# Rotary embedding on one core: the sum of the two products moves from VectorE to TensorE and ScalarE, and all x transfers become whole 4 MB chunks

## The chip, the core and the metric

The kernel runs on one core of a Trainium2 chip. The metric is the device time of one execution in microseconds. A profile of one execution is at hand; its span runs from the first to the last instruction, and the execution's own time is a little longer than the span.

## The reference

The kernel applies rotary position embedding to x of shape (16, 512, 1024), float32, with 16 heads of 64 numbers each. cos and sin have the shape (512, 32) and are shared by all batches and heads.

```python
x = x.reshape(batch, seq, num_heads, head_dim)
x1, x2 = x[..., :half_dim], x[..., half_dim:]
cos = cos[None, :, None, :]; sin = sin[None, :, None, :]
rotated = concatenate([x1*cos - x2*sin, x1*sin + x2*cos], axis=-1)
```

Input and output are 33.5 MB each.

## The kernel before

**Tiling.** A *unit* is one sequence row per partition: 128 partitions x 1024 numbers (16 heads x 2 halves x 32), 512 KB. There are 64 units. A *group* `g` is four batches; within it each partition holds `R = 16` consecutive sequence rows of one batch. Units are loaded and stored in *chunks* of 1, 2, 4 or 8 units: the first group is cut 1, 1, 2, 4, 8, the last 8, 4, 2, 1, 1, those between 8, 8, so there are 14 chunks. A chunk of n units is one DMA with n x 4 KB contiguous bytes per partition.

**Ring.** `x_sb` holds 40 units. The result overwrites x in place, and the store goes out of the same slots. The loads are issued from SP's queue (L86), which waits, before a load into used slots, for the store that empties them (L85). The stores are issued from ACT's queue (L101).

**Work of a unit.** Three steps, on two engines:

- GpSimd (POOL) multiplies the swapped halves of x by the table of -sin and +sin into `t2_sb`, one instruction for each half (L121, 128x512). `t2_sb` has `NT2 = 4` buffers.
- VectorE (DVE) multiplies x by cos into PSUM, `t1_ps` with `NT1 = 3` slots (L147, 128x1024).
- VectorE adds the two products back into x's place in SBUF (L160, 128x1024). It lags the cosine product by `LEAD = 2` units, in the written order of the loop at the end.

**Tables.** cos and sin are loaded into `stage` from ACT's queue (L90, L91). ScalarE spreads the sine table over the partitions (L97, L98), and VectorE the cosine table into PSUM (L134).

**Order.** The order on each engine is the written one. Engines are kept in step by semaphores alone: `sem_in[c]` (chunk c has landed), `sem_p` (POOL's product), `sem_m` (cosine product), `sem_v` (the sum, which frees buffers and releases stores) and `sem_out[c]` (chunk c is stored).

Of the kernel before, what the change touches and what calls it, by code (L numbers as in the profile page):

```python
# [6 lines left out]
def bass_split_heads_rope_kernel(  # L7
    nc: bass.Bass,
    x: bass.AP,
    cos: bass.AP,  # L10
    sin: bass.AP,
    num_heads: bass.AP,
    out: bass.AP,
):

    batch, seq, dim = x.shape
    H = int(num_heads)
    HD = dim // H  # L20
    HALF = HD // 2
    P = 128
    R = 16
    SB = seq // R
    BL = P // SB
    G = batch // BL
    assert SB * R == seq and BL * SB == P and G * BL == batch and SB == 32

    fp32 = mybir.dt.float32
    mult = mybir.AluOpType.mult  # L30
    add = mybir.AluOpType.add
    COPY = mybir.ActivationFunctionType.Copy


    sizes = [[1, 1, 2, 4, 8]] + [[8, 8]] * (G - 2) + [[8, 4, 2, 1, 1]]
    RING = 40
    chunks = []
    at = 0
    for g, ss in enumerate(sizes):
        r = 0  # L40
        for n in ss:
            slot = at % RING
            assert slot + n <= RING
            chunks.append((g, r, n, slot, at))
            r += n
            at += n
        assert r == R
    NC = len(chunks)
    NU = at
    unit_chunk = []  # L50
    for c, (_, _, n, _, _) in enumerate(chunks):
        unit_chunk += [c] * n

    NT1 = 3
    NT2 = 4

    with ExitStack() as stack:  # L57
        x_sb = stack.enter_context(nc.sbuf_tensor([P, RING, H, 2, HALF], fp32))
        t2_sb = stack.enter_context(nc.sbuf_tensor([P, NT2, H, 2, HALF], fp32))
        stage = stack.enter_context(nc.sbuf_tensor([SB, 2, R * HALF], fp32))  # L60
        s_sb = stack.enter_context(nc.sbuf_tensor([P, R, 2, HALF], fp32))
        c_ps = stack.enter_context(nc.psum_tensor([P, R, HALF], fp32))
        t1_ps = stack.enter_context(nc.psum_tensor([P, NT1, 2 * H, HALF], fp32))
        sem_in = [stack.enter_context(nc.semaphore(f"in{c}")) for c in range(NC)]
        sem_out = [stack.enter_context(nc.semaphore(f"out{c}")) for c in range(NC)]
        sem_cos = stack.enter_context(nc.semaphore("cos"))
        sem_sin = stack.enter_context(nc.semaphore("sin"))
        sem_c = stack.enter_context(nc.semaphore("ctab"))
        sem_s = stack.enter_context(nc.semaphore("stab"))
        sem_p = stack.enter_context(nc.semaphore("pool"))  # L70
        sem_m = stack.enter_context(nc.semaphore("mul"))
        sem_v = stack.enter_context(nc.semaphore("comb"))
        block = stack.enter_context(nc.Block(no_gpsimd_drain=False))

        xv = x.rearrange("(g b) (s r) d -> g (b s) r d", b=BL, r=R)
        ov = out.rearrange("(g b) (s r) h d -> g (b s) r (h d)", b=BL, r=R)
        xs = x_sb[:].rearrange("p n h t d -> p n (h t d)")

        @block.sync
        def _(sp):  # L80
            for c, (g, r, n, slot, at) in enumerate(chunks):
                for e, (_, _, m, eslot, eat) in enumerate(chunks):
                    if eat < at and eat + RING >= at and eslot < slot + n and slot < eslot + m:
                        if eat + RING < at + n and eat + m + RING > at:
                            sp.wait_ge(sem_out[e], 16)  # L85
                sp.dma_start(xs[:, slot:slot + n, :], xv[g, :, r:r + n, :]).then_inc(sem_in[c], 16)  # L86

        @block.scalar
        def _(ae):
            ae.dma_start(stage[:, 0, :], cos.rearrange("(s r) d -> s (r d)", r=R)).then_inc(sem_cos, 16)  # L90
            ae.dma_start(stage[:, 1, :], sin.rearrange("(s r) d -> s (r d)", r=R)).then_inc(sem_sin, 16)  # L91
            ae.wait_ge(sem_sin, 16)
            sv = stage[:, 1, :].rearrange("s (r d) -> s r d", d=HALF)
            for lo, hi in ((0, 4), (4, R)):
                for q in range(BL):
                    ps = slice(q * SB, (q + 1) * SB)
                    ae.activation(s_sb[ps, lo:hi, 0, :], sv[:, lo:hi, :], COPY, scale=-1.0)  # L97
                    ae.activation(s_sb[ps, lo:hi, 1, :], sv[:, lo:hi, :], COPY).then_inc(sem_s, 1)  # L98
            for c, (g, r, n, slot, at) in enumerate(chunks):
                ae.wait_ge(sem_v, at + n)  # L100
                ae.dma_start(ov[g, :, r:r + n, :], xs[:, slot:slot + n, :]).then_inc(sem_out[c], 16)  # L101
            for c in range(NC):
                ae.wait_ge(sem_out[c], 16)

        @block.gpsimd
        def _(pl):
            for u in range(NU):
                c = unit_chunk[u]
                g, r0, n, slot, at = chunks[c]
                r = r0 + u - at  # L110
                k = slot + u - at
                if u == at:
                    pl.wait_ge(sem_in[c], 16)
                if u == 0:
                    pl.wait_ge(sem_s, BL)  # L115
                if r == 4 and g == 0:
                    pl.wait_ge(sem_s, 2 * BL)
                if u >= NT2:
                    pl.wait_ge(sem_v, u - NT2 + 1)
                for t in range(2):  # L120
                    ins = pl.tensor_tensor(  # L121
                        t2_sb[:, u % NT2, :, t, :],
                        x_sb[:, k, :, 1 - t, :],
                        s_sb[:, r, None, t, :].broadcast_to([P, H, HALF]),
                        mult,
                    )
                ins.then_inc(sem_p, 1)

        @block.vector
        def _(ve):  # L130
            ve.wait_ge(sem_cos, 16)
            cv = stage[:, 0, :].rearrange("s (r d) -> s r d", d=HALF)
            for q in range(BL):
                ins = ve.tensor_copy(c_ps[q * SB:(q + 1) * SB, :, :], cv)  # L134
            ins.then_inc(sem_c, 1)
            ve.wait_ge(sem_c, 1)

            def mul(u):
                c = unit_chunk[u]
                g, r0, n, slot, at = chunks[c]  # L140
                r = r0 + u - at
                k = slot + u - at
                if u == at:
                    ve.wait_ge(sem_in[c], 16)
                if u >= NT1:
                    ve.wait_ge(sem_v, u - NT1 + 1)
                ve.tensor_tensor(  # L147
                    t1_ps[:, u % NT1, :, :],
                    x_sb[:, k, :, :, :].rearrange("p h t d -> p (h t) d"),
                    c_ps[:, r, None, :].broadcast_to([P, 2 * H, HALF]),  # L150
                    mult,
                ).then_inc(sem_m, 1)

            def comb(u):
                c = unit_chunk[u]
                g, r0, n, slot, at = chunks[c]
                k = slot + u - at
                ve.wait_ge(sem_m, u + 1)
                ve.wait_ge(sem_p, u + 1)  # L159
                ve.tensor_tensor(  # L160
                    x_sb[:, k, :, :, :].rearrange("p h t d -> p (h t) d"),
                    t1_ps[:, u % NT1, :, :],
                    t2_sb[:, u % NT2, :, :, :].rearrange("p h t d -> p (h t) d"),
                    add,
                ).then_inc(sem_v, 1)

            LEAD = 2
            for u in range(NU + LEAD):
                if u < NU:
                    mul(u)  # L170
                if u >= LEAD:
                    comb(u - LEAD)


# [31 lines left out]
```

## Time and profile before

| | |
|---|---|
| Time, median of 3 runs | 170.08 us (169.92 to 170.42) |
| Profiled execution: time, span | 170.16 us, 168.3 us |
| VectorE busy | 154.8 us, 92% |
| GpSimd busy | 155.7 us, 92% |
| ScalarE busy | 7.1 us, 4% |
| DMA moved | 67.27 MB, mean 400 GB/s |

Shares are of the span. In the profile, DVE is VectorE, POOL is GpSimd, ACT is ScalarE, PE is TensorE and SP is SyncE; a name with a q (ACTq) is that engine's sequencer, which issues DMAs. A row of a group of instructions reads: line, engine, operation, output and inputs with their shapes, count | busy time in us, mean ns of one | idle time of the engine before them and what ended it. The digits of a row over 40 equal slices are busy tenths.

### The profile page before, as it was taken

How to read it: one execution, taken by the hardware profiler on the slowest of the kernel's cores; microseconds unless marked ns; L12 is line 12 of the kernel's file. 1: busy time of each engine (PE TensorE's matmuls, PEld its weight loads, DVE VectorE, ACT ScalarE, POOL GpSimd, SP SyncE). 2: the span in 40 equal slices, each digit the busy share in tenths (PEclk: the TensorE clock that was granted, in tenths of full speed). 3: DMA queues.
4: the chain of work that ended last, by engine and by line, in shares of the span. 5: the costliest groups of instructions: out<-in, count | busy, mean ns of one | idle time of the engine just before them, and what ended most of it. 6: DMA issues, size and time to landing. Idle time of an engine off the chain costs nothing.

```text
span 168.3 us, 434 instructions
## 1 busy us (share of the span) xinstructions
DVE 154.8 (92%) x132; ACT 7.1 (4%) x17; POOL 155.7 (92%) x132
## 2 busy tenths in 40 slices
DVE  0999989999999999999999999999999999999942
ACT  3580000000000000000000000000000000000000
POOL 0099999999999999999999999999999999999990
DMA  5999999999999999999999999999999992289895
GB/s 149 415 432 441 438 411 462 429 421 440 407 436 440 442 444 422 413 420 350 444 428 444 428 428 444 409 428 459 426 409 457 414 442 115 125 374 492 378 400 227
DMA packets 4131, 67.27 MB, mean 400 GB/s; under 512 B 480, under 2 KB 480, under 8 KB 1568
## 3 DMA queue, kind: packets, MB, share of 16 engines
q1 hardware_dynamic: 2016, 33.56, 47.5%
q10 hardware_dynamic: 2112, 33.69, 47.0%
q14 instruction: 3, 0.02, 0.0%
HBM read 33.69 MB, written 33.55 MB: 399 GB/s over the span
## 4 chain that ended last, share of the span: by engine, by line
POOL 86%; issue 6%; DMA 3%; POOLq 1%; ACT 1%; DVE 1%; ACTq 0%; DVEq 0%
POOL t_sb L121 86%; DMA stage<-in_sin_dram 3%; POOLq L57 1%; ACT s_sb L97 1%; DVE x_sb L160 1%; ACT s_sb L98 0%; ACTq L90 0%; DVEq L159 0%; POOLq L115 0%
## 5 line engine op out<-in xcount | busy, mean ns | idle before, releaser
L121 POOL TENSOR_TENSOR t_sb<-x_sb,s_sb 128x512 f32<-128x512 f32 x128 | 155.5, 1311 | 7.9 <-ACT s_sb L98 7.9
L147 DVE TENSOR_TENSOR t_ps<-x_sb,c_ps 128x1024 f32<-128x1024 f32 x64 | 78.5, 1229 | 3.4 <-DMA x_sb<-in_x_dram 0.6
L160 DVE TENSOR_TENSOR x_sb<-t_ps,t_sb 128x1024 f32<-128x1024 f32 x64 | 78.2, 1221 | 2.5 <-POOL t_sb L121 2.5
L134 DVE COPY c_ps<-stage 32x512 f32<-32x512 f32 x4 | 2.8, 689 | 4.5 <-DMA stage<-in_cos_dram 4.5
L97 ACT ACTIVATE s_sb<-stage 32x128 f32<-32x128 f32 (+1 forms) x8 | 3.3, 415 | 3.4 <-DMA stage<-in_sin_dram 3.2
L98 ACT ACTIVATE s_sb<-stage 32x128 f32<-32x128 f32 (+1 forms) x8 | 3.2, 398 | 0.0
L97 ACT ACT_TABLE_LOAD x1 | 1.3, 1283 | 1.6 <-PEq L188 1.6
L188 POOL MEMSET const-float32-0.0<- 128x1 f32 x1 | 0.1, 98 | 0.2 <-issue 0.2
L188 POOL MEMSET const-bfloat16-1.0<- 128x1 bf16 x1 | 0.1, 102 | 0.0
L188 POOL MEMSET const-uint8-127<- 128x1 uint8 x1 | 0.1, 102 | 0.0
L188 POOL MEMSET const-float32-1.0<- 128x1 f32 x1 | 0.1, 98 | 0.0
## 6 DMA issues: line engine op xcount, KB each, us to landing
x_sb<-in_x_dram SPq DMA_DIRECT2D x6, 4096.0 KB, 30.3
out_dram<-x_sb ACTq DMA_DIRECT2D x6, 4096.0 KB, 25.1
x_sb<-in_x_dram SPq DMA_DIRECT2D x2, 2048.0 KB, 17.7
out_dram<-x_sb ACTq DMA_DIRECT2D x2, 2048.0 KB, 20.3
x_sb<-in_x_dram SPq DMA_DIRECT2D x4, 512.0 KB, 22.6
x_sb<-in_x_dram SPq DMA_DIRECT2D x2, 1024.0 KB, 18.9
out_dram<-x_sb ACTq DMA_DIRECT2D x4, 512.0 KB, 9.4
out_dram<-x_sb ACTq DMA_DIRECT2D x2, 1024.0 KB, 17.8
```

The source lines that it names most:

```text
L57: with ExitStack() as stack:
L97: ae.activation(s_sb[ps, lo:hi, 0, :], sv[:, lo:hi, :], COPY, scale=-1.0)
L98: ae.activation(s_sb[ps, lo:hi, 1, :], sv[:, lo:hi, :], COPY).then_inc(sem_s, 1)
L121: ins = pl.tensor_tensor(t2_sb[:, u % NT2, :, t, :], x_sb[:, k, :, 1 - t, :], s_sb[:, r, None, t, :].broadcast_to([P, H, HALF]), mult,)
L134: ins = ve.tensor_copy(c_ps[q * SB:(q + 1) * SB, :, :], cv)
L147: ve.tensor_tensor(t1_ps[:, u % NT1, :, :], x_sb[:, k, :, :, :].rearrange("p h t d -> p (h t) d"), c_ps[:, r, None, :].broadcast_to([P, 2 ...
L160: ve.tensor_tensor(x_sb[:, k, :, :, :].rearrange("p h t d -> p (h t) d"), t1_ps[:, u % NT1, :, :], t2_sb[:, u % NT2, :, :, :].rearrange("p ...
L188: nc = _bacc.Bacc("TRN2", target_bir_lowering=False, num_devices=1)
```

## The change

- `R` becomes 8. There are eight groups of two batches, and each group is one chunk of eight units: 8 loads and 8 stores of 4 MB, each with 32 KB contiguous per partition. Group boundaries no longer have small chunks.
- The sum is no longer an instruction of VectorE. TensorE multiplies the sine product by an identity matrix, in two matmuls of 128x512 with fp32 operands, without the flag that starts an accumulation, so that its output is added onto the cosine product that VectorE wrote to PSUM. For that the `has_written` bits of these PSUM banks have to be set: six matmuls at the beginning write all six banks once.
- ScalarE copies the sum from PSUM to x's place in SBUF, and goes on issuing the stores.
- The sine product of units 0, 2, 3, 5 and 7 of each eight is GpSimd's, now one instruction of 128x1024; that of units 1, 4 and 6 is VectorE's, from a sine table of its own in PSUM. `t2_sb` gets six buffers.
- A PSUM slot is free for the next cosine product when ScalarE has copied it (`sem_a`); a `t2_sb` buffer when TensorE has added it (`sem_e`).
- The tables: 64 partitions of 1 KB instead of 32 of 2 KB. VectorE makes its two tables in six instructions after both loads have landed.

```diff
-    R = 16
+    R = 8
-    sizes = [[1, 1, 2, 4, 8]] + [[8, 8]] * (G - 2) + [[8, 4, 2, 1, 1]]
+    sizes = [[R]] * G
     RING = 40
+    on_pool = [u % 8 in (0, 2, 3, 5, 7) for u in range(NU)]
     NT1 = 3
-    NT2 = 4
+    NT2 = 6
@@ scalar
             for c, (g, r, n, slot, at) in enumerate(chunks):
-                ae.wait_ge(sem_v, at + n)
+                for i in range(n):
+                    u = at + i
+                    ae.wait_ge(sem_e, u + 1)
+                    ae.activation(xs[:, slot + i, :], t1_ps[:, u % NT1, :], COPY).then_inc(sem_a, 1)
+                ae.wait_ge(sem_a, at + n)
                 ae.dma_start(ov[g, :, r:r + n, :], xs[:, slot:slot + n, :]).then_inc(sem_out[c], 16)
@@ tensor (new)
+            pe.wait_ge(sem_i, 2)
+            for k in range(NT1):
+                for b in range(EH):
+                    pe.matmul(
+                        t1_ps[:, k, b * BANK:(b + 1) * BANK],
+                        ident[:],
+                        ident[:, None, :].broadcast_to([P, BANK // P, P]),
+                        start=True,
+                        stop=True,
+                    ).then_inc(sem_w, 1)
+            for u in range(NU):
+                pe.wait_ge(sem_m, u + 1)
+                if on_pool[u]:
+                    pe.wait_ge(sem_p, n_pool[u])
+                else:
+                    pe.wait_ge(sem_d, n_dve[u])
+                t2 = t2_sb[:, u % NT2, :, :, :].rearrange("p h t d -> p (h t d)")
+                for b in range(EH):
+                    ins = pe.matmul(
+                        t1_ps[:, u % NT1, b * BANK:(b + 1) * BANK],
+                        ident[:],
+                        t2[:, b * BANK:(b + 1) * BANK],
+                        start=False,
+                        stop=True,
+                        skip_group_check=True,
+                    )
+                ins.then_inc(sem_e, 1)
@@ gpsimd
+            pl.memset(ident[:], 1.0).then_inc(sem_i, 1)
...
+                if not on_pool[u]:
+                    continue
+                pl.wait_ge(sem_in[c], 16)
                 if u >= NT2:
-                    pl.wait_ge(sem_v, u - NT2 + 1)
-                for t in range(2):
...
+                    pl.wait_ge(sem_e, u - NT2 + 1)
+                pl.tensor_tensor(
+                    t2_sb[:, u % NT2, :, :, :], swapped(k), sin_of(s_sb, r), mult
+                ).then_inc(sem_p, 1)
@@ vector
+            ve.wait_ge(sem_sin, 16)
             for q in range(BL):
+                ps = slice(q * SB, (q + 1) * SB)
+                ve.tensor_copy(c_ps[ps, :, :], cv)
+                ve.tensor_scalar_mul(s_ps[ps, :, 0, :], sv, -1.0)
+                ve.tensor_copy(s_ps[ps, :, 1, :], sv).then_inc(sem_c, 1)
+            ve.wait_ge(sem_w, NT1 * EH)
+            for u in range(NU):
+                c, r, k, first = where(u)
+                if first:
                     ve.wait_ge(sem_in[c], 16)
+                if not on_pool[u]:
+                    if u >= NT2:
+                        ve.wait_ge(sem_e, u - NT2 + 1)
+                    ve.tensor_tensor(
+                        t2_sb[:, u % NT2, :, :, :], swapped(k), sin_of(s_ps, r), mult
+                    ).then_inc(sem_d, 1)
                 if u >= NT1:
-                    ve.wait_ge(sem_v, u - NT1 + 1)
+                    ve.wait_ge(sem_a, u - NT1 + 1)
                 ve.tensor_tensor(  (the cosine product, as before)
-            def comb(u):  (the add onto x_sb, removed)
```

More of the change, by code (lines that the diff above doesn't have):

```diff
@@ L26, in bass_split_heads_rope_kernel @@
     G = batch // BL
-    assert SB * R == seq and BL * SB == P and G * BL == batch and SB == 32
+    assert SB * R == seq and BL * SB == P and G * BL == batch
     fp32 = mybir.dt.float32
     mult = mybir.AluOpType.mult
-    add = mybir.AluOpType.add
     COPY = mybir.ActivationFunctionType.Copy
-    sizes = [[1, 1, 2, 4, 8]] + [[8, 8]] * (G - 2) + [[8, 4, 2, 1, 1]]
+    sizes = [[R]] * G
     RING = 40
@@ L52, in bass_split_heads_rope_kernel, with where @@
         unit_chunk += [c] * n
+    def where(u):
+        c = unit_chunk[u]
+        g, r0, n, slot, at = chunks[c]
+        return c, r0 + u - at, slot + u - at, u == at
+    on_pool = [u % 8 in (0, 2, 3, 5, 7) for u in range(NU)]
+    n_pool = [sum(on_pool[: u + 1]) for u in range(NU)]
+    n_dve = [u + 1 - n_pool[u] for u in range(NU)]
     NT1 = 3
-    NT2 = 4
+    NT2 = 6
+    BANK = 512
+    EH = H * HD // BANK
     with ExitStack() as stack:
@@ L61, in bass_split_heads_rope_kernel @@
         s_sb = stack.enter_context(nc.sbuf_tensor([P, R, 2, HALF], fp32))
-        c_ps = stack.enter_context(nc.psum_tensor([P, R, HALF], fp32))
-        t1_ps = stack.enter_context(nc.psum_tensor([P, NT1, 2 * H, HALF], fp32))
+        ident = stack.enter_context(nc.sbuf_tensor([P, P], fp32))
+        tab_ps = stack.enter_context(nc.psum_tensor([P, 2, BANK], fp32))
+        t1_ps = stack.enter_context(nc.psum_tensor([P, NT1, H * HD], fp32))
         sem_in = [stack.enter_context(nc.semaphore(f"in{c}")) for c in range(NC)]
@@ L77, in bass_split_heads_rope_kernel, with swapped, sin_of @@
         xs = x_sb[:].rearrange("p n h t d -> p n (h t d)")
+        def swapped(k):
+            return x_sb[:, k, :, ::-1, :]
+        def sin_of(table, r):
+            return table[:, r, None, :, :].broadcast_to([P, H, 2, HALF])
         @block.sync
@@ L81, in _ @@
             for c, (g, r, n, slot, at) in enumerate(chunks):
[L82 to L85, printed above, removed]
+                for e, (_, _, m, _, eat) in enumerate(chunks):
+                    if eat + RING < at + n and eat + m + RING > at:
+                        sp.wait_ge(sem_out[e], 16)
                 sp.dma_start(xs[:, slot:slot + n, :], xv[g, :, r:r + n, :]).then_inc(sem_in[c], 16)
@@ L93, in _ @@
             sv = stage[:, 1, :].rearrange("s (r d) -> s r d", d=HALF)
[L94 to L98, printed above, removed]
-            for c, (g, r, n, slot, at) in enumerate(chunks):
-                ae.wait_ge(sem_v, at + n)
+            for q in range(BL):
+                ps = slice(q * SB, (q + 1) * SB)
+                ae.activation(s_sb[ps, :, 0, :], sv, COPY, scale=-1.0)
+                ae.activation(s_sb[ps, :, 1, :], sv, COPY).then_inc(sem_s, 1)
+            for c, (g, r, n, slot, at) in enumerate(chunks):
+                for i in range(n):
[3 more added lines that the diff above has]
+                ae.wait_ge(sem_a, at + n)
                 ae.dma_start(ov[g, :, r:r + n, :], xs[:, slot:slot + n, :]).then_inc(sem_out[c], 16)
@@ L103, in _ @@
                 ae.wait_ge(sem_out[c], 16)
+        @block.tensor
+        def _(pe):
+            pe.wait_ge(sem_i, 2)
[25 more added lines that the diff above has]
+                ins.then_inc(sem_e, 1)
@@ L105, in _ @@
         @block.gpsimd
         def _(pl):
-            for u in range(NU):
[L108 to L117, printed above, removed]
-                if u >= NT2:
-                    pl.wait_ge(sem_v, u - NT2 + 1)
-                for t in range(2):
[L121 to L127, printed above, removed]
+            pl.memset(ident[:], 1.0).then_inc(sem_i, 1)
@@ L131, in _ @@
             ve.wait_ge(sem_cos, 16)
+            ve.wait_ge(sem_sin, 16)
             cv = stage[:, 0, :].rearrange("s (r d) -> s r d", d=HALF)
+            sv = stage[:, 1, :].rearrange("s (r d) -> s r d", d=HALF)
             for q in range(BL):
[L134 to L143, printed above, removed]
-                    ve.wait_ge(sem_in[c], 16)
+                ps = slice(q * SB, (q + 1) * SB)
+                ve.tensor_copy(c_ps[ps, :, :], cv)
+                ve.tensor_scalar_mul(s_ps[ps, :, 0, :], sv, -1.0)
+                ve.tensor_copy(s_ps[ps, :, 1, :], sv).then_inc(sem_c, 1)
+            ve.wait_ge(sem_c, BL)
+            ve.wait_ge(sem_w, NT1 * EH)
+            for u in range(NU):
+                c, r, k, first = where(u)
+                if first:
+                    ve.wait_ge(sem_in[c], 16)
+                if not on_pool[u]:
[4 more added lines that the diff above has]
+                    ).then_inc(sem_d, 1)
                 if u >= NT1:
-                    ve.wait_ge(sem_v, u - NT1 + 1)
+                    ve.wait_ge(sem_a, u - NT1 + 1)
                 ve.tensor_tensor(
-                    t1_ps[:, u % NT1, :, :],
+                    t1_ps[:, u % NT1, :].rearrange("p (h d) -> p h d", d=HALF),
                     x_sb[:, k, :, :, :].rearrange("p h t d -> p (h t) d"),
@@ L152, in mul @@
                 ).then_inc(sem_m, 1)
[L154 to L172, printed above, removed]
 _INS = ['x', 'cos', 'sin', 'num_heads']
```

19 lines of the change are left out of this document (18 added, 1 removed).

## The prediction

> **What bounds the kernel now.** I read the page first, then the chain of waits in order of time, then the table of stretches. In the page, DVE and POOL are the product and add engines, and the two DMA queues are q10 (loads) and q1 (stores).
>
> ```profile
> span 168.3 us, 434 instructions
> ...
> DVE 154.8 (92%) x132; ACT 7.1 (4%) x17; POOL 155.7 (92%) x132
> ...
> DMA  5999999999999999999999999999999992289895
> ...
> DMA packets 4131, 67.27 MB, mean 400 GB/s; under 512 B 480, under 2 KB 480, under 8 KB 1568
> ...
> q1 hardware_dynamic: 2016, 33.56, 47.5%
> q10 hardware_dynamic: 2112, 33.69, 47.0%
> ...
> POOL 86%; issue 6%; DMA 3%; POOLq 1%; ACT 1%; DVE 1%; ACTq 0%; DVEq 0%
> ...
> L121 POOL TENSOR_TENSOR t_sb<-x_sb,s_sb 128x512 f32<-128x512 f32 x128 | 155.5, 1311 | 7.9 <-ACT s_sb L98 7.9
> L147 DVE TENSOR_TENSOR t_ps<-x_sb,c_ps 128x1024 f32<-128x1024 f32 x64 | 78.5, 1229 | 3.4 <-DMA x_sb<-in_x_dram 0.6
> L160 DVE TENSOR_TENSOR x_sb<-t_ps,t_sb 128x1024 f32<-128x1024 f32 x64 | 78.2, 1221 | 2.5 <-POOL t_sb L121 2.5
> ```
>
> Three resources are nearly full: POOL and DVE at 92%, and the DMA engines at 47.5 + 47.0 = 94.5%, that is 159 us of 168.3. The chain that ended last runs 86% through POOL. Its pieces give POOL's pace:
>
> ```profile
> 42.36 18.52 POOL t_sb L121 x16
> 60.88 0.90 issue
> 61.78 18.41 POOL t_sb L121 x16
> ```
>
> Sixteen instructions are eight units (one unit is 128 x 1024 numbers, two POOL instructions): 18.5 + 0.9 = 19.4 us, 2.43 us per unit. DVE does two instructions per unit, 1.229 + 1.221 = 2.45 us. So both engines go at the same pace. The stretches show what that costs (columns: length, then busy time of DVE, ACT and POOL, granted TensorE clock, DMA share, GB/s):
>
> ```profile
> 1.00:2.00 1.00, 0.00 (x0) 0.36 (x1) 0.00 (x0) 1.00 0.43 53
> 2.00:3.00 1.00, 0.00 (x0) 0.92 (x1) 0.00 (x0) 1.00 0.71 154
> 3.00:4.00 1.00, 0.00 (x0) 0.00 (x0) 0.00 (x0) 1.00 0.93 346
> 12.00:20.00 8.00, 7.79 (x8) 0.07 (x1) 8.00 (x8) 1.00 1.03 443
> 40.00:140.00 100.00, 98.25 (x84) 0.00 (x0) 100.00 (x83) 1.00 1.00 427
> 135.00:145.00 10.00, 9.79 (x9) 0.00 (x0) 10.00 (x9) 1.00 0.53 227
> 150.00:155.00 5.00, 4.86 (x5) 0.00 (x0) 5.00 (x5) 1.00 0.99 421
> ```
>
> From 3 to about 137 us the DMA engines are full at 427 GB/s or more. Only near 135 to 150 us, with all loads done, do they wait for POOL and DVE to hand over the next chunk. That hole is nearly all that separates the span from a pure transfer time: a faster compute side can save the hole and no more.
>
> **The change part by part.**
> *DVE.* The add of L160 goes (64 x 1.221 us). 24 of the 64 units (three of eight) get their sine product on DVE, same shape and the same kind of operands (one SBUF, one PSUM) as L147, so 24 x 1.229. New sum 88 x 1.229 = 108 us, or 1.69 us per unit.
> *POOL.* 40 of 64 units stay, each one 128x1024 instruction for two 128x512. I take twice the pitch of L121, 2 x 18.52/16 = 2.32 us, so 93 us, or 1.45 per unit on average. Its wait is now on TensorE's progress five units back; six buffers cover that.
> *ACT.* It copies each 128x1024 sum from PSUM. The price comes from its shapes:
>
> ```profile
> L97 ACT ACTIVATE s_sb<-stage 32x384 f32<-32x384 f32 x4 | 2.1, 522 | 0.1
> L97 ACT ACTIVATE s_sb<-stage 32x128 f32<-32x128 f32 x4 | 1.2, 308 | 3.3 <-DMA stage<-in_sin_dram 3.2
> L134 DVE COPY c_ps<-stage 32x512 f32<-32x512 f32 x4 | 2.8, 689 | 4.5 <-DMA stage<-in_cos_dram 4.5
> ```
>
> (522 - 308)/256 = 0.836 ns per element, so 522 + 640 x 0.836 = 1.06 us, 68 us in all, 1.06 per unit. The store issues stay on ACT's queue, and a wait of the next store there now holds back the copies behind it; each issue is 0.34 us (rows below), eight of them, hidden because ACT has 0.6 us spare per unit.
> *TensorE.* Two 128x512 matmuls per unit. No row of this trace shows one; the granted clock of 1.00 stands over an idle engine. Lower bound: the fastest streaming shown, ACT's slope, 1024 x 0.836 = 0.86 us per unit. Upper: POOL's 2.43. I take the row of the very work it replaces, the add of L160, 1.22 us. The chain of one PSUM slot (1.23 + 1.22 + 1.06 = 3.5 us over three slots) is then no limit, and DVE sets the pace at 1.69 to 1.75 us per unit. The Trainium skill, "FP8 and Floating Point Precision", TensorE Precision Notes, says that true fp32 takes four passes; with the 2.4 GHz of "TensorE: Matmul & The Clock Gate" (Part 1) my estimate is 2 x 4 x 512/2.4 = 1.71 us per unit, which would leave the sum as it is. No run here shows it.
> *The six seeding matmuls* run while the first chunk loads; cover some 13 us. If each cost the upper bound's half, 1.2 us, they take 7.
> *The loads and tables.* Every packet is now 32 KB (8 rows of 4 KB, contiguous). What that does to the small table loads I read from the early stores, 4 KB packets amid loads of 32 KB packets; the next rows are issues (count, KB each, median us to landing), then single issues (start, length), the first compute of DVE among them:
>
> ```profile
> out_dram<-x_sb ACTq DMA_DIRECT2D x2, 512.0 KB, 19.5
> out_dram<-x_sb ACTq DMA_DIRECT2D x1, 4096.0 KB, 31.1
> out_dram<-x_sb ACTq DMA_DIRECT2D x1, 4096.0 KB, 31.2
> out_dram<-x_sb ACTq DMA_DIRECT2D x1, 4096.0 KB, 28.2
> stage<-in_sin_dram ACTq DMA_DIRECT2D x1, 64.0 KB, 4.9
> ```
> ```profile
> 1.16 0.45 ACTq L91 DMA_DIRECT2D stage<-in_sin_dram  x1
> 7.28 3.49 DVE L147 TENSOR_TENSOR t_ps<-x_sb,c_ps 128x1024 f32<-128x1024 f32 x3
> 12.20 2.79 ACTq L101 DMA_DIRECT2D out_dram<-x_sb  x2
> 48.92 0.34 ACTq L101 DMA_DIRECT2D out_dram<-x_sb  x1
> 68.10 0.34 ACTq L101 DMA_DIRECT2D out_dram<-x_sb  x1
> 87.45 0.34 ACTq L101 DMA_DIRECT2D out_dram<-x_sb  x1
> ```
>
> One engine moves 427/16 = 26.7 GB/s, a 32 KB packet in 1.23 us, a 4 KB one in 0.15. If packets of the two queues alternate, a 512 KB store (8 packets and a completion per engine) takes 9 x 1.38 = 12.4 us, the second behind it 24.8; less the 2.4 us between their issues the mean is 17.4, and about 1.4 us of latency makes 18.8 against 19.5 shown. So they alternate. Each table is 64 rows of 1 KB: 4 packets and a completion, 5 x 1.27 = 6.3 us; both are through some 13 us after 2 us, sin at about 15.5 us instead of 1.16 + 4.9 = 6.1. Six DVE table instructions of 256 elements (slope from 689 and 1229 ns: 1.05 ns, so 0.42 us each) end at 18: compute starts there, not at 7.3. Cover: five chunks of loads are queued and keep the DMA engines full till past 50 us. Bounds for sin: 6 us, as before, or 24 (ten slots of 2.2 us, if the 19.5 us were those of one store's nine). At 24, compute starts at 27 and chunk 7 is ready at 27 + 64 x 1.72 + 3 = 140, still ahead of its store (below).
>
> **The sum,** by bytes. A chunk is 4.19 MB: 9.8 us alone at 427 GB/s, 19.6 beside a stream of equal share. Traffic in the first 4 us is 0.55 MB, so the stream starts, in effect, at 2.7 us. Chunk 0 is computed at 18 + 8 x 1.72 + 3 (the depth of the pipeline) = 35. Loads had the engines alone till then: 3.3 chunks. The other 4.7 take 4.7 x 19.6 = 92, to 127. Chunk 5 needs store 0 (done 55, the queue gets there at 68), chunk 6 store 1 (74, at 88), chunk 7 store 2 (94, at 107): no ring wait. 3.3 chunks of stores are left at 127, 32 us: 160. The last store can start at 150; chunk 7 is computed at 128 + 14 + 3 = 145, so 5 us to spare. All bytes at one rate say the same: 67.24 MB / 427 = 157.5, + 2.7 = 160.2. After the last byte come about 1 us of landing and 0.5 us to the end:
>
> ```profile
> out_dram<-x_sb ACTq DMA_DIRECT2D x2, 512.0 KB, 3.1
> 165.00:168.30 3.30, 0.21 (x1) 0.00 (x0) 0.00 (x0) 1.00 0.44 176
> ```
>
> Span 161.7. The profiled execution took 170.16 us, 1.86 over its span and 0.08 over the median of 170.08. 161.7 + 1.86 = 163.5 us, 3.9% less. At the 443 GB/s of the loads alone it would be 158; at the 421 of the stores alone, 166.
>
> **The rivals.**
> *TensorE above the pace.* If compute is the limit, the span is 18 + 64c + 3 + 9.8 + 1.5 = 32.3 + 64c, since the whole first chunk lies open at the start and the whole last store at the end. It passes 161.7 at c = 2.02 us per unit and the old span at 2.13. For: the upper bound, 2.43, gives 188 + 2 = 190 us; chunks of eight make head and tail larger than before (compute at 18 instead of 7.3, a last store of 9.8 us instead of 3.1). Against: TensorE would have to be 1.7 times slower than the DVE add it replaces. This ends slower. Chance 0.16, a third of it between 2.02 and 2.13.
> *Half the clock.* The same mechanism with another cause: chunks arrive every 19.6 us and need 14, so TensorE idles 5 us in each, and if the granted clock falls in such gaps and does not come back, 1.22 becomes 2.44 and the time 190. If it does come back within some 3 us of work, each chunk loses a few us that the 5 us of slack cover. Nothing in the profile speaks on it. "TensorE: Matmul & The Clock Gate" of the Trainium skill (Part 1) says that the clock halves after about 3.4 us idle and returns after about as much work, and that it has been seen stuck low for over 50 us; with my four-pass estimate the stuck case would be 3.41 us per unit and 252 us. Chance 0.07.
> *Stores outrun loads.* By the rows above the store issued at 48.92 landed at 80.0, that of 68.10 at 99.3, that of 87.45 at 115.7: 19.3 and 16.4 us for a chunk, the second 60% of the rate. If stores took 60% all along, the loads' 4.7 chunks would take 24.5 us each, chunk 7 would land at 150 and be computed at 167, the last store would go out with nothing beside it, and the time is 167 + 11.3 + 1.9 = 180. At 55% it is 168. It decides from the point where chunk 7 is ready after 150, at 52%. For: one of the two intervals. Against: the other, which is an even share. Chance 0.09, a third of it the full case.
> *It does not raise the DMA's mean.* The hole goes, another comes at the start, since the first store waits for a chunk: 168 to 170 us. Against: loads fill that time. Chance 0.04.
>
> **How the numbers follow.** 0.64 for 163.5 us (own range 161 to 167). The range 161 to 180 leaves out a TensorE price over 2.28 us (0.06), the clock that stays at half (0.06), the end of the stores' rival (0.02) and what is under 161 (0.05). Faster by over 0.3% (the runs of before spread 169.92 to 170.42, so less cannot be told): 0.64, 0.05 of the first rival and 0.05 of the third, 0.74. Within 0.3%: 0.04, from the last rival and the crossing of the first. Slower: 0.22.
>
> **What would show it.** Right: DMA row full to the last slice, 1152 packets on q1 (8 x 144), stores in 20 us steps from about 35 us, DVE near 108 us, POOL near 93, ACT near 70 with its copies near 1.06 us, sin landing at 13 to 17 us, and DVE, POOL and TensorE idle between chunks for loads. Wrong: TensorE near 100% busy with DVE waiting for ACT and ACT for TensorE; a granted clock under 1; a hole in the DMA row before the last store.

## The result and the profile after

The changed kernel took 163.48 us (median of four runs, 162.8 to 164.68) against 170.12 before: a ratio of 0.9616, 95% interval 0.9546 to 0.9685. The forecast was 163.5 us. A second set of six runs on another occasion (experiment 8) gave a median of 165.02 us, 162.79 to 166.57, and a ratio of 0.9656 (0.9615 to 0.9698). The two longest of the six, 165.43 and 166.57, lie over 1.5% above the fastest and count as slow runs, so the ratio leaves them out; the other four have a median of 164.78. The profiled execution is the longest of the first four runs: it took 164.68 us at a span of 163.0.

The page of the changed kernel (PE is TensorE, PEld its weight loads; the rows over 40 slices are busy tenths, PEclk the granted clock):

```profile
span 163.0 us, 904 instructions
...
PE 122.4 (75%) x268; PEld 53.0 (33%) x268; DVE 104.1 (64%) x94; ACT 68.2 (42%) x69; POOL 94.0 (58%) x46
...
PE   6920069999999999999999999926999199950000
...
PEclk9995557999999999999999999997899999998555
DMA  6999999999999999999999999999999999999992
...
DMA packets 2469, 67.30 MB, mean 413 GB/s; under 512 B 288, under 2 KB 416, under 8 KB 416
...
q1 hardware_dynamic: 1152, 33.55, 49.1%
q10 hardware_dynamic: 1312, 33.69, 48.3%
...
PE t_ps L154 56%; DMA stage<-in_sin_dram 10%; POOL t_sb L185 8%; ACT x_sb L128 1%; ACT s_sb L122 1%; ACT s_sb L123 0%; ACTq L116 0%; POOLq L184 0%
...
L154 PE MATMUL t_ps<-t_sb,ident 128*128 128x512 f32 x256 | 114.7, 611 | 20.8 <-POOL t_sb L185 20.8
L185 POOL TENSOR_TENSOR t_sb<-x_sb,s_sb 128x1024 f32<-128x1024 f32 x40 | 93.3, 2361 | 45.1 <-DMA x_sb<-in_x_dram 19.7
L128 ACT ACTIVATE x_sb<-t_ps 128x1024 f32<-128x1024 f32 x64 | 65.5, 1023 | 61.0 <-PE t_ps L154 61.0
L214 DVE TENSOR_TENSOR t_ps<-x_sb,tab_ps 128x1024 f32<-128x1024 f32 x64 | 76.9, 1226 | 19.9 <-ACT x_sb L128 11.1
L209 DVE TENSOR_TENSOR t_sb<-x_sb,tab_ps 128x1024 f32<-128x1024 f32 x24 | 29.1, 1214 | 0.0
```

The DMA row is the one to read: 9 in every slice from the second to the last but one. The two digits of 2 that the kernel before had near the end are gone, and the queues' shares rose to 49.1 + 48.3 = 97.4% of a shorter span. Over the whole span no engine is nearly full any more, but TensorE is busy in nine tenths or more of each slice from about 24 to 106 us. The chain of waits puts 56% on TensorE and 10% on the sine load; experiments 3 and 5 show that neither costs time.

The timeline of the changed kernel has the stores' issues (start, length) and VectorE's wait for the last chunk:

```profile
39.21 0.35 ACTq L130 DMA_DIRECT2D out_dram<-x_sb  x1
52.94 0.34 ACTq L130 DMA_DIRECT2D out_dram<-x_sb  x1
...
128.08 0.34 ACTq L130 DMA_DIRECT2D out_dram<-x_sb  x1
128.15 1.23 DVE L214 TENSOR_TENSOR t_ps<-x_sb,tab_ps 128x1024 f32<-128x1024 f32 x1 [3.98 <-DMA x_sb<-in_x_dram]
...
145.75 0.34 ACTq L130 DMA_DIRECT2D out_dram<-x_sb  x1
```

From one store to the next 13.73 us pass as long as chunks lie ready: 1.717 us per unit. Chunk 7 landed at 128 us and was ready at 145.75, where the forecast had 127 to 128 and 145.

### The profile page after: what moved, and what is told of

Read it like the earlier page. It is cut to its first block, busy times and chain, and to the rows that moved or that the text cites. A ratio compares the mean times of both kernels' runs of the same rounds, so it can differ in the third digit from the quotient of the medians.

```text
span 163.0 us, 904 instructions
## 1 busy us (share of the span) xinstructions
PE 122.4 (75%) x268; PEld 53.0 (33%) x268; DVE 104.1 (64%) x94; ACT 68.2 (42%) x69; POOL 94.0 (58%) x46
## 3 DMA queue, kind: packets, MB, share of 16 engines
q1 hardware_dynamic: 1152, 33.55, 49.1%
q10 hardware_dynamic: 1312, 33.69, 48.3%
## 4 chain that ended last, share of the span: by engine, by line
PE 56%; issue 13%; DMA 10%; POOL 8%; ACT 2%; ACTq 0%; POOLq 0%
PE t_ps L154 56%; DMA stage<-in_sin_dram 10%; POOL t_sb L185 8%; ACT x_sb L128 1%; ACT s_sb L122 1%; ACT s_sb L123 0%; ACTq L116 0%; POOLq L184 0%
## 5 line engine op out<-in xcount | busy, mean ns | idle before, releaser
L154 PE MATMUL t_ps<-t_sb,ident 128*128 128x512 f32 x256 | 114.7, 611 | 20.8 <-POOL t_sb L185 20.8
L185 POOL TENSOR_TENSOR t_sb<-x_sb,s_sb 128x1024 f32<-128x1024 f32 x40 | 93.3, 2361 | 45.1 <-DMA x_sb<-in_x_dram 19.7
L128 ACT ACTIVATE x_sb<-t_ps 128x1024 f32<-128x1024 f32 x64 | 65.5, 1023 | 61.0 <-PE t_ps L154 61.0
L214 DVE TENSOR_TENSOR t_ps<-x_sb,tab_ps 128x1024 f32<-128x1024 f32 x64 | 76.9, 1226 | 19.9 <-ACT x_sb L128 11.1
L154 PEld LDWEIGHTS t_ps<-t_sb,ident 128*128 128x128 f32 x256 | 49.8, 196 | 85.7 <-issue 64.9
L209 DVE TENSOR_TENSOR t_sb<-x_sb,tab_ps 128x1024 f32<-128x1024 f32 x24 | 29.1, 1214 | 0.0
L197 DVE COPY tab_ps<-stage 64x256 f32<-64x256 f32 x2 | 0.8, 424 | 17.8 <-DMA stage<-in_sin_dram 17.8
L139 PE MATMUL t_ps<-ident 128*128 128x512 f32 x12 | 7.7, 812 | 1.4 <-POOL ident L168 1.4
L122 ACT ACTIVATE s_sb<-stage 64x256 f32<-64x256 f32 x2 | 0.8, 416 | 14.4 <-DMA stage<-in_sin_dram 14.4
L139 PEld LDWEIGHTS t_ps<-ident 128*128 128x128 f32 x12 | 3.1, 270 | 5.2 <-issue 3.8
L199 DVE COPY tab_ps<-stage 64x256 f32<-64x256 f32 x2 | 0.8, 414 | 0.0
L123 ACT ACTIVATE s_sb<-stage 64x256 f32<-64x256 f32 x2 | 0.8, 398 | 0.0
## 6 DMA issues: line engine op xcount, KB each, us to landing
stage<-in_sin_dram ACTq DMA_DIRECT2D x1, 64.0 KB, 16.3
```

Source lines behind the costliest of these rows:

```text
L122: ae.activation(s_sb[ps, :, 0, :], sv, COPY, scale=-1.0)
L123: ae.activation(s_sb[ps, :, 1, :], sv, COPY).then_inc(sem_s, 1)
L128: ae.activation(xs[:, slot + i, :], t1_ps[:, u % NT1, :], COPY).then_inc(sem_a, 1)
L139: pe.matmul(t1_ps[:, k, b * BANK:(b + 1) * BANK], ident[:], ident[:, None, :].broadcast_to([P, BANK // P, P]), start=True, stop=True,).the ...
L154: ins = pe.matmul(t1_ps[:, u % NT1, b * BANK:(b + 1) * BANK], ident[:], t2[:, b * BANK:(b + 1) * BANK], start=False, stop=True, skip_group ...
L185: pl.tensor_tensor(t2_sb[:, u % NT2, :, :, :], swapped(k), sin_of(s_sb, r), mult).then_inc(sem_p, 1)
```

## The experiments

Theory: the DMA engines, with 67 MB at a nearly fixed rate, set the end, and the pace of compute matters only past a turning point, a time per unit above which compute is no longer hidden behind the transfers. Rivals: the larger packets bring the gain by themselves; TensorE or the sine load sets the time, as the chain says; the open head and tail of 4 MB chunks cost time.

**1. The chunks alone, with the old compute.**

```diff
-    R = 16
+    R = 8
-    sizes = [[1, 1, 2, 4, 8]] + [[8, 8]] * (G - 2) + [[8, 4, 2, 1, 1]]
+    sizes = [[R]] * G
```

> The kernel of before with nothing but R = 8 and chunks of eight units throughout; VectorE still adds, GpSimd still does all sine products. Theory (the DMA engines set the end, and the compute pace decides only whether it stays hidden): the pace is still 2.43 us per unit, now with the whole first chunk open at the start and the whole last store open at the end, so GpSimd starts at about 18.5 us (sine table behind 32 KB packets), 18.5 + 64 x 2.43 + 2.5 + 0.5 + 9.8 + 1.5 = 188, time 190 us, slower than before. Rival (the larger packets themselves bring the gain, TensorE's part is beside the point): 163 to 165 us.

189.32 us, ratio 1.1118 (1.1100 to 1.1137). The chain in order of time (start, length), and two stretches (length, busy time of DVE, ACT, POOL, clock, DMA share, GB/s):

```profile
33.48 18.45 POOL t_sb L121 x16
51.93 0.93 issue
```
```profile
30.00:140.00 110.00, 108.01 (x92) 0.00 (x0) 110.00 (x91) 1.00 0.94 401
140.00:170.00 30.00, 29.52 (x26) 0.00 (x0) 30.00 (x26) 1.00 0.57 245
```

The pace is still 18.45 + 0.93 = 19.4 us for eight units, and the DMA engines stand over 40% idle at the end (share 0.57). The whole chunks alone lose 19 us: they are only bearable with a pace clearly under 2.43 us. The new compute does not need them in turn (experiment 4).

**2. The floor: a bare copy through the same ring.** All compute and both tables are left out; each chunk is stored as it landed.

```diff
 (ScalarE, for each chunk)
-    (wait for TensorE and copy the sum, eight times; wait for the copies)
+    ae.wait_ge(sem_in[c], 16)
     ae.dma_start(ov[g, :, r:r + n, :], xs[:, slot:slot + n, :]).then_inc(sem_out[c], 16)
```

> No compute and no tables at all: the same eight loads and eight stores through the same ring, each store as soon as its chunk has landed (the output is x itself). Theory: this is the floor of the changed kernel, 67.1 MB at 427 GB/s = 157.2, + 2.7 to the first byte + 1.5 + 1.9 = 163 us, within 1 us of the changed kernel. Rival (some of the changed kernel's time is still compute, table loading or the wait for the sine table on the chain): 3 us or more below it, 155 to 160 us.

161.48 us, 0.9486 (0.9471 to 0.9501). The changed kernel is 2.0 us above this floor by its first set of runs and 3.3 by the four runs of the second, the kernel before was 8.6. The expectation of 163 us was 1.5 us too high. Its "within 1 us of the changed kernel" did not come, and neither did the rival's 155 to 160, though the distance that the rival named, 3 us or more, is met by the second set. So all but 2 to 3 us is accounted for by the transfers; experiment 7 looks for the rest.

**3. The tables ahead of x.**

```diff
         def _(sp):
+            sp.dma_start(stage[:, 0, :], cos...).then_inc(sem_cos, 16)
+            sp.dma_start(stage[:, 1, :], sin...).then_inc(sem_sin, 16)
             (the loads of x)
         def _(ae):
-            (the same two loads)
```

> The changed kernel with the cosine and sine loads issued from SP's queue ahead of all loads of x, instead of from ACT's queue beside them. Theory: the tables land at about 4 to 5 us instead of 11.5 and 17.7, compute starts when chunk 0 lands (about 14 us instead of 19.3), the first store goes out some 4 us earlier, and the time does not change (within 1 us, perhaps 1 us more because x starts after two more issues), since the DMA engines are full all the while. Rival (the chain that ended last is right to show 10% on the sine load): 4 us or more faster.

163.77 us, 0.9622 (0.9605 to 0.9640): no change. The issue rows (KB, us to landing) of the changed kernel, then of this one, and this one's first store:

```profile
stage<-in_sin_dram ACTq DMA_DIRECT2D x1, 64.0 KB, 16.3
```
```profile
stage<-in_sin_dram SPq DMA_DIRECT2D x1, 64.0 KB, 2.2
```
```profile
35.20 0.38 ACTq L130 DMA_DIRECT2D out_dram<-x_sb  x1
```

The sine load took 2.2 us instead of 16.3 and the first store went out 4 us earlier. The end did not move. The 10% of the chain was a wait beside full DMA engines.

**4. Small chunks at both ends.**

```diff
-    sizes = [[R]] * G
+    sizes = [[1, 1, 2, 4]] + [[8]] * (G - 2) + [[4, 2, 1, 1]]
```

> The changed kernel with small chunks at both ends as the kernel of before had them: the first eight units as 1, 1, 2, 4 and the last eight as 4, 2, 1, 1. Theory: the tables land early again (small packets beside them), compute starts at about 8 us, the last store is 512 KB, and the time does not change beyond 1 us, since the bytes and their rate are the same; if anything 0 to 2 us slower, as small packets take fewer bytes per turn. Rival (the open head and tail of 4 MB chunks cost time): about 5 to 10 us faster.

165.74 us, 0.9728 (0.9711 to 0.9744): 2.3 us above the changed kernel's first set and 1 us above the four runs of its second, with an interval outside both. That is at or just past the far end of the theory's range, and not the rival's gain. Against the kernel before it is still 4.6 us faster, with chunks at both ends as small as there: the new compute brings most of the gain by itself, and whole chunks add the last 1 to 2 us. The issues in the stretch from 90 to 125 us, then the last unit on the timeline:

```profile
x_sb<-in_x_dram SPq DMA_DIRECT2D x1, 2048.0 KB, 23.3
x_sb<-in_x_dram SPq DMA_DIRECT2D x1, 1024.0 KB, 35.0
x_sb<-in_x_dram SPq DMA_DIRECT2D x2, 512.0 KB, 49.5
```
```profile
153.69 2.34 POOL L185 TENSOR_TENSOR t_sb<-x_sb,s_sb 128x1024 f32<-128x1024 f32 x1 [17.30 <-DMA x_sb<-in_x_dram]
156.17 3.75 PE L154 MATMUL t_ps<-t_sb,ident 128*128 128x512 f32 x4 [5.22 <-POOL t_sb L185]
161.01 0.34 ACTq L130 DMA_DIRECT2D out_dram<-x_sb  x1
```

The four loads were issued one after the other within 2 us, so each figure includes the wait for those ahead of it on the queue. The last ones, of 4 KB packets, run beside stores of 32 KB packets: the last 512 KB land at about 153.6 us, some 9 us after the 512 KB before them (VectorE starts on these two units at 144.92 and 153.64), where 512 KB alone would take an estimated 1.2 us at 427 GB/s. What follows lies open: GpSimd's product, TensorE at half the clock after its idle time (3.75 us for a unit that takes 1.72), the copy, the store. The small last chunk did not help here.

**5. TensorE made dearer.** A third matmul per unit, with an all-zero weight matrix, adds nothing to the sum but time.

```diff
+                ins = pe.matmul(t1_ps[:, u % NT1, 0:K], zero[:], t2[:, 0:K],
+                                start=False, stop=True, skip_group_check=True)
                 ins.then_inc(sem_e, 1)
```

With K = 64 columns:

> The changed kernel with a third matmul per unit on TensorE, an all-zero weight matrix with 64 columns of the sine product, so nothing changes in the sum. TensorE's price per unit was 1.717 us (four records of 0.429) and becomes about 1.717 x (1 + 64/1024) = 1.82 us. Theory: with TensorE as the pace, chunk 7 is ready at 21.7 + 64c + 3.7 (the first units at half clock) + 1.1, and the last store could start at about 150 us; so c up to about 1.93 is hidden. 1.82 is below: 163.5 us, no change. Rival (TensorE, 75% busy and 56% of the chain that ended last, sets the time): 64 x 0.107 = 6.8 us more, 170 us.

With K = 256:

> The same with 256 columns: c = 1.717 x 1.25 = 2.15 us, above the turning point of 1.93. Theory: span 21.7 + 64 x 2.15 + 3.7 + 1.1 + 9.8 + 1.5 = 175.4, time 177 us, slower than before. Prediction's own turning point (2.02) would give 32.3 + 64 x 2.15 + 1.9 = 172. Rival (every added matmul counts in full): 163.5 + 64 x 0.43 = 191 us.

With K = 512:

> The same with 512 columns: c = 2.575 us. Theory: 37.8 + 64 x 2.575 + 1.9 = 204.5 us, that is 64 x 0.43 = 27 us over the run with 256 columns. Rival (every added matmul counts in full): 163.5 + 64 x 0.858 = 218 us.

163.85 us, 0.9623 (0.9592 to 0.9653); 176.46 us, 1.0330 (1.0274 to 1.0386); 203.94 us, 1.1961 (1.1934 to 1.1988). The rival, by which every added matmul counts in full, had 170, 191 and 218 us. The timeline of the run with 64 columns shows that its pace was not 1.82 but 1.94 us per unit, and its last store went out at 148.5 (its issue row is the last):

```profile
135.81 1.02 ACT L129 ACTIVATE x_sb<-t_ps 128x1024 f32<-128x1024 f32 x1 [0.92 <-PE t_ps L163]
137.75 1.02 ACT L129 ACTIVATE x_sb<-t_ps 128x1024 f32<-128x1024 f32 x1 [0.92 <-PE t_ps L163]
...
148.50 0.34 ACTq L131 DMA_DIRECT2D out_dram<-x_sb  x1
```

So 64 x 0.22 = 14 us of TensorE time were added and cost nothing that can be told from the changed kernel's runs. Above the turning point all counts: from 256 to 512 columns the time rose by 27.5 us, and 64 x 0.43 is 27.5. Going back along this line from 176.46 at c = 2.15 us (c is TensorE's time per unit), 163.5 is met at c = 2.15 - 12.96/64 = 1.95 us; with 164.8, the second set's figure, it would be 1.97. The run with 64 columns sits at this turning point. The page and the waits of the run with 256 columns (waited for: total, times, longest) show TensorE as the bound there:

```profile
PE 148.1 (85%) x396; PEld 77.1 (44%) x396; DVE 105.6 (60%) x94; ACT 68.3 (39%) x69; POOL 94.5 (54%) x47
```
```profile
ACT x_sb L129 <- PE t_ps L163: 78.3, 64, 7.2
POOL t_sb L195 <- PE t_ps L163: 38.7, 22, 2.1
DVE t_ps L224 <- ACT x_sb L129: 34.3, 38, 2.8
```

These are its three longest waits; every engine waits on TensorE, directly or through ScalarE.

**6. Chunks of four and of two units.**

```diff
-    sizes = [[R]] * G
+    sizes = [[4, 4]] * G          (and, in a second kernel, [[2, 2, 2, 2]] * G)
```

> The changed kernel with 16 chunks of four units (2 MB, 16 KB packets) instead of 8 of eight. Theory (bytes over the rate, the rate being much the same for 16 KB as for 32 KB packets): 162.5 to 164.5 us; the tables land some 4 us earlier and the last store is shorter, both hidden. Rival (the gain hangs on 32 KB packets; 16 KB ones lose 2 to 4% of the rate): 166 to 170 us.

> The changed kernel with 32 chunks of two units (1 MB, 8 KB packets) throughout. The kernel with small chunks only at its ends lost 2 us; two explanations: small packets are slow in themselves, or small packets lose their turn to large ones of the other queue. Theory (it is the mixture): with 8 KB on both queues the loads and stores share evenly, 163 to 164 us, as with 16 KB. Rival (small packets move fewer bytes per us, so this with all packets small is worse than only a few): 166 us or more, with a mean rate under 410 GB/s in the middle.

Chunks of four: 163.24 us (163.12 to 163.28), 0.9575 (0.9559 to 0.9590), the lowest median of this study among the kernels that do the whole work, though inside the interval of the changed kernel's first set. Chunks of two: 164.63 us, 0.9669 (0.9655 to 0.9683). The stretch from 40 to 100 us of the two, in that order (the busy columns are TensorE, its weight loads, DVE, ACT, POOL):

```profile
40.00:100.00 60.00, 54.83 (x128) 23.65 (x127) 50.04 (x44) 32.77 (x32) 43.13 (x20) 1.00 1.01 430
```
```profile
40.00:100.00 60.00, 53.61 (x121) 21.92 (x119) 47.25 (x41) 30.97 (x31) 40.73 (x18) 1.00 1.01 427
```

The gain does not hang on 32 KB packets: 16 KB give at least as much, with a narrower spread than the changed kernel's own. With 8 KB throughout the rate is 427 GB/s, so packets of 8 KB are not slow by themselves, and the mixture of sizes is the likelier cause of what hurt experiment 4; packets of 4 KB on both queues were not run. The time lies 0.6 us above what the theory allowed, and where that goes was not traced.

**7. What is left over the floor.** A copy as in experiment 2, and beside it the changed kernel's work on GpSimd, VectorE and TensorE, on a buffer that no transfer touches. ScalarE copies nothing, VectorE waits for TensorE's sum instead of that copy, and the output is x itself.

```diff
-            return x_sb[:, k, :, ::-1, :]
+            return y_sb[:, k % 2, :, ::-1, :]
 (the cosine product's input likewise; no waits on sem_in in the engines; tables first, as in 3; stores as in 2)
```

> What is left between the changed kernel (163.5) and the bare copy (161.5)? This kernel stores each chunk as it landed, as the bare copy does (the output is x itself), and beside it GpSimd, VectorE and TensorE do the changed kernel's work per unit on a buffer of their own that no transfer touches; ScalarE copies nothing, the tables are loaded first on SP's queue. No transfer waits for compute. Theory A (engines that read and write SBUF slow the transfers a little): GB/s some 1 to 2% lower while compute runs (to about 120 us) than afterwards, time 162.5 to 163.5 us. Theory B (the 2 us come from the tables at the start and from when the stores are handed over): the rate is the bare copy's 434 throughout and the time 161.5 to 162.3 us.

164.11 us, 0.9649 (0.9631 to 0.9668): 0.6 us above the range of theory A and without the lower rate that it forecast. The stretch from 60 to 110 us of this kernel, then of the bare copy:

```profile
60.00:110.00 50.00, 50.00 (x118) 22.11 (x117) 46.09 (x41) 0.00 (x0) 42.96 (x19) 1.00 1.00 430
```
```profile
60.00:110.00 50.00, 0.00 (x0) 1.00 1.00 430
```

In this stretch three busy engines do not slow the transfers. Nor does theory B's 161.5 to 162.3 hold. One part of B's cause does show: with the tables ahead on the same queue, this kernel's first loads of x were issued 1.3 us later than the bare copy's, half of the 2.6 us between the two. The bare copy's issues, then this kernel's:

```profile
0.73 2.44 SPq L112 DMA_DIRECT2D x_sb<-in_x_dram  x5
```
```profile
2.03 2.29 SPq L116 DMA_DIRECT2D x_sb<-in_x_dram  x4
```

The changed kernel has its tables on the other queue and starts its loads at 0.80 us, so this is not what it loses. Its last stretches and those of the bare copy differ:

```profile
158.00:161.00 3.00, 0.00 (x0) 0.00 (x0) 0.00 (x0) 0.00 (x0) 0.00 (x0) 0.50 0.63 273
150.00:158.00 8.00, 0.00 (x0) 0.00 (x0) 0.00 (x0) 0.00 (x0) 0.00 (x0) 0.50 0.96 414
```
```profile
156.00:159.00 3.00, 0.00 (x0) 1.00 0.81 350
150.00:156.00 6.00, 0.00 (x0) 1.00 1.00 431
```

The bare copy holds 431 GB/s to within about 2.5 us of its last byte, the changed kernel is at 414 from 150 us on and at 273 in its last 3 us. Up to 150 us the two had moved nearly the same, 63.2 and 63.5 MB. Why the end of the transfers is thinner was not settled; the last 2 to 3 us stay open.

**8. Two together, and the changed kernel once more.** The first has chunks of four and the tables first; the second is the changed kernel itself.

> The two variants that did not lose, together: chunks of four units and the tables ahead of x on SP's queue. Theory (all of that is hidden behind the transfers): 163 to 164 us, no gain over 163.2. Rival (each hides a little of its own): 161.5 to 162.5 us.

> The changed kernel itself, for a narrower interval and as the yardstick on the same chip: 163 to 164 us. Its four runs so far lay at 162.8 (twice), 164.1 and 164.7; if that spread comes from when loads and stores happen to meet, it stays as wide here, and the kernel with chunks of four has less of it.

164.51 us, 0.9660 (0.9648 to 0.9673), 0.5 us above the theory's range: no gain from joining them, rather a loss of about 0.9% against chunks of four alone (0.9660 to 0.9575; the two were run on different chips). The changed kernel: 165.02 us, 164.78 by the four of the ratio, above the 163 to 164 that were expected. Those four go from 162.79 to 165.23 and the first set from 162.8 to 164.68, so the spread came back; chunks of four stayed within 0.2 us in their one set. What causes the spread was not traced.

## Why the prediction was right, point by point

- *The bound.* Predicted: a faster compute side can save the hole near the end and no more. The DMA row is full, the bare copy at 161.48 us lies close below, and adding 14 us to TensorE changed nothing that can be told. The sum's rate of 427 GB/s stands beside the copy's 430.
- *The size, and luck in it.* The same sum gave 163 us for the bare copy, 1.5 too much. It also has nothing for the 2 to 3 us that the changed kernel takes over that copy. The two errors are of opposite sign, and that the forecast met the first median to 0.1 us is their near cancelling; against the second set it is 1.3 to 1.5 us low.
- *VectorE, GpSimd, ScalarE.* Predicted 108, 93 and 68 us busy; the page of the profile has 104.1, 94.0 and 68.2. The durations 1.226, 2.361 and 1.023 us answer to 1.229, 2.32 and 1.06. VectorE's rows add up to 108 as well; its busy time is less because instructions that follow one another overlap in the records.
- *TensorE.* This term was mis-sized: 1.22 us per unit was taken from the add that it replaces, 1.717 was measured. "FP8 and Floating Point Precision", TensorE Precision Notes, of the Trainium skill has four passes for true fp32, and the estimate of 1.71 us from that agrees with the trace to 0.01 us. It did no harm, because 1.717 is only just above VectorE's forecast 1.69 and under the turning point, but it changed which engine sets the pace of compute: not VectorE, as the sum had it, but TensorE. That 1.717 falls into the 1.69 to 1.75 us given for VectorE is a coincidence.
- *The turning point.* Predicted at 2.02 us per unit, measured at 1.95, that is 64 x 0.07 or some 4.5 us more lying open. Two missing pieces are at the start: compute began at 20.0 us and not at 18, and the first units ran at half the clock. From TensorE's first sum to the store the first chunk took 17.5 us (21.74 to 39.21), the last chunk, all at full clock, 15.1 (130.69 to 145.75): 2.4 us.
- *Half the clock.* The rival's mechanism exists and stays small. The gaps it counted on before every chunk came only before the last two, since the loads had run ahead of compute until then. These stretches of the changed kernel show the clock (the third number from the right) fall some 4 us after the seeding matmuls end at 9.2 us, and come back 5 us after work starts at 21.74:

```profile
12.00:13.00 1.00, 0.00 (x0) 0.00 (x0) 0.00 (x0) 0.00 (x0) 0.00 (x0) 0.97 1.19 454
13.00:14.00 1.00, 0.00 (x0) 0.00 (x0) 0.00 (x0) 0.00 (x0) 0.00 (x0) 0.50 0.45 174
...
25.00:26.00 1.00, 1.00 (x2) 0.34 (x1) 0.00 (x0) 0.47 (x1) 1.00 (x1) 0.50 1.21 524
26.00:27.00 1.00, 1.00 (x3) 0.53 (x2) 0.42 (x1) 0.55 (x1) 1.00 (x2) 0.70 1.22 524
27.00:28.00 1.00, 1.00 (x3) 0.38 (x2) 1.00 (x2) 0.14 (x1) 1.00 (x1) 1.00 1.07 459
```

  TensorE's stretches of the changed kernel, then one of experiment 3 (start, length, idle time before):

```profile
21.74 85.05 PE L154 MATMUL t_ps<-t_sb,ident 128*128 128x512 f32 x192 [12.59 <-POOL t_sb L185]
111.32 15.67 PE L154 MATMUL t_ps<-t_sb,ident 128*128 128x512 f32 x32 [4.54 <-POOL t_sb L185]
130.69 13.97 PE L154 MATMUL t_ps<-t_sb,ident 128*128 128x512 f32 x32 [3.70 <-POOL t_sb L185]
```
```profile
91.53 15.55 PE L154 MATMUL t_ps<-t_sb,ident 128*128 128x512 f32 x32 [2.50 <-POOL t_sb L185]
```

  The same 32 records took 13.97 us after a gap of 3.70 us and 15.67 after one of 4.54, and in experiment 3 15.55 after one of 2.50: the clock fell in or just after two of these gaps (it stood at 0.50 from 112 to 115 us and, in experiment 3, from 92 to 94) and not in the third, at a cost of 1.6 to 1.7 us each. "TensorE: Matmul & The Clock Gate" of the Trainium skill (Part 1) gives at least one window of about 3.4 us for both directions; the stretches above, with 4 to 5, agree, and experiment 3's fall, after 2.50 us of idle time, came sooner. In this trace the clock always came back. The stuck clock that the Trainium skill tells of there is at a quarter, so the forecast's 252 us, worked out at half, is not its price; no run here shows it.
- *The sine table.* Predicted at 15.5 us by packets that take turns, landed at 17.7; compute began at 20.0 instead of 18. Hidden, as predicted (experiment 3).
- *Stores outrun loads.* Chunk 7 landed at 128 us, as an even share gives; not at the 150 of that rival.
- *The signs it named.* Right: the full DMA row, 1152 packets on q1, the busy times. Not as named: the first six stores were issued 13.73 us apart and not 20, and compute idled for loads only before the last two chunks. Two of its signs of being wrong appeared all the same: a granted clock under 1 (mean 0.906), and, from 24 to 106 us, TensorE full with VectorE waiting for ScalarE and ScalarE for TensorE. They meant no loss, because 1.717 us per unit is still faster than the 19.6 us per chunk, 2.45 per unit, at which loads arrive beside stores. Only the third sign, a hole in the DMA row before the last store, would have told, and it stayed away.
- *What was not foreseen.* The spread of the changed kernel's runs, and the 2 to 3 us over the floor.

## What to carry to other kernels

Ask first what the transfers alone would take; a copy through the same buffers measures it in one run, and the distance to it is the most that compute can give back. Then look for the pace per unit at which compute stops being hidden, with the first chunk's load and the last chunk's store lying open: under it, even 14 us more on the engine that leads the chain of waits cost nothing; above it every microsecond counts. Where two DMA queues take turns, look at their packet sizes: here the queue with the small packets fell behind, while equal packets of 32, 16 and 8 KB all ran at 427 to 431 GB/s in the stretches shown of the bare copy and of experiment 6.

## What the runs showed of the hardware that was not expected

- Beside 32 KB-packet stores, 512 KB of load in 4 KB packets landed some 9 us after the load ahead of them, and a 64 KB table took 16.3 us beside 32 KB-packet loads instead of 2.2 ahead of them. The prediction used such turns for the tables; what they do to small chunks at the end showed in experiment 4.
- A matmul of 64 columns added 0.22 us per unit where a share by columns is 0.107, while one of 256 added its full share of 0.43: small fp32 matmuls seem to have a floor (one size was tried, and whether the matmul or its weight loads set it was not separated).
- The granted clock can fall in or just after the gaps between chunks too, once after as little as 2.50 us of idle time, and the next chunk then starts at half speed: in experiment 4 this lengthened the exposed last unit by 2 us.
